# Routing wholly on VectorE in paced pieces, gate products over 48 instead of 64 tiles, and every fourth one-hot row made by ScalarE, in a two-layer float32 block

## The chip, the cores and the metric

The kernel runs on one core of a Trainium2 chip. The metric is the device time of one execution in microseconds. The kernel before was timed three times: 1633.87, 1632.1 and 1633.6 us, a median of 1633.6. A profiled execution took 1632.75 us, and its span from the first to the last instruction is 1631.0 us. All times of the trace below are counted from the start of that span.

## The reference, cut to what matters

Two layers over 256 frames of width 1024, all in float32. The change touches the PEER part of the first layer, in which each frame picks 16 of 16384 single-neuron experts for each of 8 heads:

```python
def peer(x, w_q, sub_k1, sub_k2, expert_u, expert_v):
    q = (xt @ w_q).reshape(T, 8, 2, 128)
    s1 = einsum('thd,kd->thk', q[:, :, 0], sub_k1)      # 128 scores per head and side
    s2 = einsum('thd,kd->thk', q[:, :, 1], sub_k2)
    v1, i1 = top_k(s1, 16); v2, i2 = top_k(s2, 16)
    cand = (v1[..., :, None] + v2[..., None, :])        # 16 x 16 sums
    vals, ci = top_k(cand, 16)
    idx = i1[ci // 16] * 128 + i2[ci % 16]              # the chosen experts
    gates = softmax(vals)
    h = einsum('tkd,td->tk', expert_u[idx], x)
    a = gelu(h) * gates
    return einsum('tk,tkd->td', a, expert_v[idx])
```

## The kernel before

**Dense experts.** No expert is gathered. The kernel computes the hidden value of all 16384 experts for all 256 frames, as 128 tiles of 128 experts, and multiplies it with a gate matrix that is zero wherever an expert was not chosen. The up pass (tile `ps_u`, lines 575 to 577) takes one weight tile of 128x1024 from memory for each expert tile; the down pass (`acc_v`, line 605) follows with another 128 weight tiles.

**Split weights.** Each float32 weight tile is split into a rounded high part `wh` (ScalarE, line 63) and the rest `wl` (VectorE, line 69), and three matmuls of 256 columns are made for each of 8 slices: 24 matmuls for an expert tile. `Stream.get` issues the split of the tile two places ahead at the start of a tile; the buffer for it comes free when TensorE has finished the tile before.

**Routing.** `route` (lines 1101 to 1161) is a generator. After each up tile `pump` runs it to its next `yield`, twice after every fourth tile. It makes the top 16 of each side (`top16`, lines 1083 to 1098, with VectorE's MAX8, FIND_INDEX8 and MATCH_REPLACE8), the top 16 of 50 candidate sums, and then, for each block of 128 frames, turns the candidate number into the two key numbers with one-hot arrays of 128x2048 elements: a comparison, a product and a sum for each. Three of these products are on GpSimd (lines 1135, 1141 and 1148), the rest is on VectorE. The first key number is a sum over slots of differences (`d1`); a separate sum (`base`, lines 1135 and 1144) gives the start of the slot. Two transposes (`jtp`, line 1158) and a copy (line 1159) give `jt`: first key number, second key number and gate of each choice, with a column for each frame. The scratch of the routing lies in `ha1` and `ha2`, the arrays that later hold the hidden values (rows 0 to 111 and 112 to 127).

**Gates.** A frame's gate matrix (128x128) is the product of two one-hot arrays, `o1` (scaled by the gate, VectorE, line 1179) and `o2` (GpSimd, line 1178). `g_step` handles four frames: `apply` multiplies the product of the step before into the hidden values that exist already (VectorE, line 1199) and copies the rest to where later hidden values will be (ScalarE, line 1201); `products` makes four float32 products (TensorE, line 1187) from the one-hot arrays of the step before; `build` makes the next four pairs of one-hot arrays. One `g_step` stands behind each up tile, so 256 frames take 64 tiles. `epilogue`, at the start of a tile, applies gelu to the tile before (ScalarE, lines 1209 and 1212) and multiplies the part whose gates are there (VectorE, line 1213).

**Order.** Nothing reorders these: each engine runs its instructions in the order in which the code above emits them, and semaphores alone hold it up. An up tile therefore emits, in this order, the split of the tile two ahead (lines 63, 69), the epilogue of the tile before, its 24 matmuls, a gate step, and a piece of the routing.

Of the kernel before, what the change touches and what calls it, by code (L numbers as in the profile page):

```python
# [15 lines left out]
ALU = mybir.AluOpType  # L16
# [147 lines left out]
class Kern:  # L164
# [404 lines left out]
    def mm_wstat(self, ps, w, xh, xl, nk=8, off=0):  # L569
# [375 lines left out]
    def experts(self, second):  # L945
# [11 lines left out]
        with tc.tile_pool(name="ha", bufs=1, side="right") as hp:  # L957
# [28 lines left out]
            self.bg.append(self.route(s, rb, self.slots, self.jt))  # L986
# [51 lines left out]
    def scores(self, xh, xl, kt, qt, s):  # L1038
# [16 lines left out]
        for side in range(2):  # L1055
            for h in range(4 - 4 * side, 8):
# [17 lines left out]
                self.pump()  # L1074
# [8 lines left out]
    def top16(self, jobs):  # L1083

        nc = self.nc
        for v, sc, ov, oi in jobs:
            nc.vector.max(ov[:, 0:8], v)
        for v, sc, ov, oi in jobs:
            nc.vector.max_index(oi[:, 0:8], ov[:, 0:8], v)
        for v, sc, ov, oi in jobs:  # L1090
            nc.vector.match_replace(sc, ov[:, 0:8], v, -3.0e38)
        yield
        for v, sc, ov, oi in jobs:
            nc.vector.max(ov[:, 8:16], sc)
        for v, sc, ov, oi in jobs:
            nc.vector.max_index(oi[:, 8:16], ov[:, 8:16], sc)
        yield

    def route(self, s, r, start, jt):
        nc = self.nc  # L1100
        for n in range(4):
            side, h0 = n // 2, 4 * (n % 2)
            while self.scored <= n:
                yield
            for b in range(NB):
                for h in range(h0, h0 + 4, 2):
                    yield from self.top16([(s[b][side][:, h + j], r["sc"][j], r["v"][b][:, side, h + j],
                                            r["iu"][b][:, side, h + j]) for j in range(2)])
        oh4 = r["oh"].rearrange("p (h k) e -> p h k e", k=16)
        oh24 = r["oh2"].rearrange("p (h k) e -> p h k e", k=16)  # L1110
        slots = lambda ap: ap[:, None, :].to_broadcast([P, P, 16])
        per = lambda ap: ap[:, :, None].to_broadcast([P, P, 16])
        for b in range(NB):
            v, fi, d1, cand = r["v"][b], r["fi"], r["d1"], r["cand"]
            for x in range(8):
                n, at = self.WIDTH[x], self.START[x]
                nc.vector.tensor_tensor(cand[:, :, at:at + n], v[:, 0, :, x:x + 1].to_broadcast([P, 8, n]),
                                        v[:, 1, :, 0:n], op=ALU.add)
            nc.vector.tensor_tensor(cand[:, :, 42:50], v[:, 0, :, 8:16], v[:, 1, :, 0:1].to_broadcast([P, 8, 8]),
                                    op=ALU.add)  # L1120
            yield
            nc.vector.tensor_copy(fi, r["iu"][b])
            nc.vector.tensor_copy(d1[:, :, 0:1], fi[:, 0, :, 0:1])
            nc.vector.tensor_tensor(d1[:, :, 1:16], fi[:, 0, :, 1:16], fi[:, 0, :, 0:15], op=ALU.subtract)
            yield
            for h in range(0, 8, 2):
                yield from self.top16([(cand[:, h + j], r["sc"][j][:, 0:50], r["cv"][:, h + j], r["ci"][:, h + j])
                                       for j in range(2)])
            g = r["out"][2].rearrange("p (h k) -> p h k", k=16)
            nc.vector.tensor_copy(r["cf"], r["ci"].rearrange("p h k -> p (h k)"))  # L1130
            nc.vector.tensor_tensor(g, r["cv"], r["cv"][:, :, 0:1].to_broadcast([P, 8, 16]), op=ALU.subtract)
            nc.scalar.activation(g, g, AF.Exp)
            yield
            nc.vector.tensor_tensor(r["oh"], per(r["cf"]), slots(start[:, 0]), op=ALU.is_ge)  # L1134
            nc.gpsimd.tensor_tensor(r["oh2"], r["oh"], slots(start[:, 1]), op=ALU.mult)  # L1135
            yield
            nc.vector.tensor_reduce(r["sm"], g, axis=AX.X, op=ALU.add)
# [11 lines left out]
            yield
            nc.vector.tensor_reduce(r["out"][0], r["oh"], axis=AX.X, op=ALU.add)  # L1150
            yield
            yield
            yield
            nc.vector.tensor_reduce(r["out"][1], r["oh2"], axis=AX.X, op=ALU.add)
            yield
            ps = self.psum("acc", f"jtp{b}", [P, 3, P])
            for j in range(3):
                nc.tensor.transpose(ps[:, j], r["out"][j], self.ident)
            nc.scalar.activation(jt[:, :, b * P:b * P + P], ps, AF.Copy)
            yield  # L1160
        self.route_done = True

    def experts_up(self, xh, xl, jt, pu):
# [61 lines left out]

        for i in range(P):
# [8 lines left out]
        self.drain()  # L1235
# [559 lines left out]
```

## Time and profile before

| what | value |
|---|---|
| median of three runs | 1633.6 us (1632.1 to 1633.87) |
| the profiled execution | 1632.75 us, span 1631.0 us |
| TensorE busy | 1583.3 us, 97% of the span |
| VectorE, ScalarE, GpSimd busy | 1121.7, 814.7 and 423.3 us |
| up tiles begin | at 254.0 us |
| gate steps, first and last product | at 437.9 and 675.2 us |
| down pass begins | at 697.7 us |

"Busy" of TensorE is a sum over pipelined matmuls and doesn't say that each of them ran at its best. What matters is where TensorE waits, for whom, and which engine's queue the work of that other engine stands behind. A profile's "idle before" in brackets is the time that an engine stood still ahead of an instruction, with the instruction whose end released it.

### The profile page before, as it was taken

The page shows a single profiled execution, that of the slowest core. Times are in us where ns is not written, and L with a number is a line of the kernel's source. Part 1 is how long each engine was busy: PE and PEld are TensorE (multiplying, and loading weights), DVE is VectorE, ACT ScalarE, POOL GpSimd, SP SyncE. Part 2 cuts the span into 40 slices and gives each one's busy share as a digit, 9 for nine tenths or more (in the row PEclk, how much of TensorE's full clock was granted, in tenths as well). Part 3 has the DMA queues.
Part 4 walks back from the last instruction along what each step waited for, and adds up shares of the span by engine and source line. Part 5 has one row for each costly group of instructions (what it writes and reads, how often), then busy time and mean ns, then how long its engine had stood idle before and what let it go on. Part 6 is the DMA issues. An engine that isn't in the chain of part 4 may idle for free.

```text
span 1631.0 us, 27358 instructions
## 1 busy us (share of the span) xinstructions
PE 1583.3 (97%) x10366; PEld 1439.3 (88%) x10366; DVE 1121.7 (69%) x2197; ACT 814.7 (50%) x1417; POOL 423.3 (26%) x462
## 2 busy tenths in 40 slices
PE   7999999989899999999999999999999989899998
PEld 6899899989899999988888888799997977689996
DVE  4477758898877788755555555755557879775555
ACT  5544545445344444455555555654446655564443
POOL 3121100041689999400000000021101574110000
PEclk9999999999999999999999999999999999999999
DMA  6555555546444444456666666566655532356563
GB/s 205 160 160 177 170 160 174 183 132 181 153 143 143 141 136 140 154 181 207 193 194 194 194 194 194 168 195 196 195 182 172 165 116 78 129 168 182 188 186 116
DMA packets 75667, 273.12 MB, mean 167 GB/s; under 512 B 8800, under 2 KB 8928, under 8 KB 75536
## 3 DMA queue, kind: packets, MB, share of 16 engines
q1 hardware_dynamic: 73728, 267.16, 52.9%
q0 software_dynamic: 1520, 3.93, 0.9%
q8 instruction: 82, 1.34, 0.3%
q14 instruction: 49, 0.40, 0.1%
q10 hardware_dynamic: 288, 0.29, 0.1%
HBM read 270.29 MB, written 1.05 MB: 166 GB/s over the span
## 4 chain that ended last, share of the span: by engine, by line
PE 87%; DVE 7%; ACT 2%; issue 2%; POOL 1%; DMA 0%; DVEq 0%; ACTq 0%
PE acc_v L605 21%; PE ps_u L577 7%; PE acc_ffn L605 7%; PE ps_u L576 7%; PE ps_u L575 7%; PE g L1187 3%; DVE wl L69 3%; PE acc_wo L605 2%; PE ffn2u L576 1%; PE ffn2u L575 1%; PE ffn2u L577 1%; PE ffn2g L576 1%; PE ffn2g L575 1%; PE ffn2g L577 1%; PE ffn1u L577 1%
## 5 line engine op out<-in xcount | busy, mean ns | idle before, releaser
L69 DVE TENSOR_TENSOR wl<-raw,wh 128x1024 fp32r<-128x1024 f32 x477 | 610.6, 1281 | 412.2 <-ACT wh L63 411.1
L63 ACT ACTIVATE wh<-raw 128x1024 fp32r<-128x1024 f32 x492 | 519.5, 1057 | 406.8 <-PE acc_v L605 166.7
L577 PE MATMUL ps_u<-xh_n,wl 128*128 128x256 f32 x1024 | 292.5, 286 | 9.6 <-DVE wl L69 9.6
L575 PE MATMUL ps_u<-xh_n,wh 128*128 128x256 f32 x1024 | 297.0, 290 | 0.0
L576 PE MATMUL ps_u<-xl_n,wh 128*128 128x256 f32 x1024 | 291.7, 285 | 0.0
L1178 POOL TENSOR_SCALAR o<-iota,jt 128x128 f32<-128x128 f32 x256 | 219.3, 872 | 29.4 <-PE g L1187 29.0
L577 PEld LDWEIGHTS ps_u<-xh_n,wl 128*128 128x128 f32 x1024 | 198.0, 193 | 10.6 <-DVE wl L69 10.6
L575 PEld LDWEIGHTS ps_u<-xh_n,wh 128*128 128x128 f32 x1024 | 198.7, 194 | 0.0
L576 PEld LDWEIGHTS ps_u<-xl_n,wh 128*128 128x128 f32 x1024 | 198.4, 194 | 0.0
L605 PE MATMUL acc_v<-wh,ah 128*128 128x512 f32 x508 | 157.6, 389 | 1.4 <-ACT ah L316 1.4
L605 PE MATMUL acc_v<-wl,ah 128*128 128x512 f32 x508 | 157.5, 389 | 0.0
L605 PE MATMUL acc_v<-wh,al 128*128 128x512 f32 x508 | 157.3, 389 | 0.0
L605 PEld LDWEIGHTS acc_v<-wh,ah 128*128 128x128 f32 x508 | 95.3, 188 | 21.3 <-ACT ah L316 1.6
L605 PEld LDWEIGHTS acc_v<-wl,ah 128*128 128x128 f32 x508 | 95.3, 188 | 19.9
L605 PEld LDWEIGHTS acc_v<-wh,al 128*128 128x128 f32 x508 | 95.3, 188 | 19.8
L362 POOL TENSOR_TENSOR ha<-res,final_g 128x512 f32<-128x512 f32 x3 | 3.9, 1293 | 311.4 <-DVE res L390 305.8
L1201 ACT ACTIVATE ha<-g 128x64 f32<-128x64 f32 (+53 forms) x118 | 22.4, 238 | 109.4 <-DVE ha L1199 109.4
L1179 DVE TENSOR_SCALAR o<-iota,jt 128x128 f32<-128x128 f32 x256 | 76.8, 363 | 0.0
L69 POOL TENSOR_TENSOR wl<-raw,wh 128x1024 fp32r<-128x1024 f32 x15 | 36.1, 2407 | 121.3 <-ACT wh L63 121.3
L1187 PE MATMUL g<-o,o 128*128 128x128 f32 x512 | 67.4, 274 | 0.0
L1187 PEld LDWEIGHTS g<-o,o 128*128 128x128 f32 x512 | 62.6, 192 | 0.0
L1135 POOL TENSOR_TENSOR ha<-ha,slots 128x2048 f32<-128x2048 f32 x2 | 10.9, 5457 | 177.1 <-DVE ha L1134 177.1
(615 smaller groups left out, 3488.2 us busy)
## 6 DMA issues: line engine op xcount, KB each, us to landing
raw<-in_u_dram SPq DMA_DIRECT2D x128, 512.0 KB, 3.5
raw<-in_v_dram SPq DMA_DIRECT2D x128, 512.0 KB, 3.5
raw<-in_ffn_gu_dram SPq DMA_DIRECT2D x88, 512.0 KB, 3.9
raw<-in_w_in_dram SPq DMA_DIRECT2D x74, 512.0 KB, 3.6
raw<-in_ffn_d_dram SPq DMA_DIRECT2D x44, 512.0 KB, 3.5
raw<-in_w_out_dram SPq DMA_DIRECT2D x20, 512.0 KB, 3.5
raw<-in_wq_dram SPq DMA_DIRECT2D x16, 512.0 KB, 3.6
raw<-in_w_ab_dram SPq DMA_DIRECT2D x8, 512.0 KB, 3.4
```

Source lines behind the costliest of these rows:

```text
L63: self.k.nc.scalar.activation(h, self.raw[i], AF.Copy)
L69: (eng or self.k.nc.vector).tensor_sub(lo, self.raw.pop(i), h.bitcast(F32))
L362: ("Pool", 1.3, lambda: nc.gpsimd.tensor_tensor(o, x, y, op=ALU.mult))], deps)
L575: nc.tensor.matmul(ps, h[:, c], xh[:, k], start=(k == 0), stop=False)
L576: nc.tensor.matmul(ps, h[:, c], xl[:, k], start=False, stop=False)
L577: nc.tensor.matmul(ps, lo[:, c], xh[:, k], start=False, stop=(k == nk - 1))
L605: nc.tensor.matmul(acc[b][hf], (ah, ah, al)[p][:, s], (h, lo, h)[p][:, c], start=first and p == 0, stop=last and p == 2)
L1135: nc.gpsimd.tensor_tensor(r["oh2"], r["oh"], slots(start[:, 1]), op=ALU.mult)
L1178: nc.gpsimd.tensor_scalar(o2[:, j], self.iota, jt[:, 1, t:t + 1], None, op0=ALU.is_equal)
L1179: nc.vector.tensor_scalar(o1[:, j], self.iota, jt[:, 0, t:t + 1], jt[:, 2, t:t + 1], op0=ALU.is_equal, op1=ALU.mult)
L1187: nc.tensor.matmul(ps[:, j], o2[:, j], o1[:, j], start=True, stop=True)
L1201: nc.scalar.activation(ha[:, m - a:e - a, t0:t0 + GB], pv[:, m:e], AF.Copy)
```

## The change

1. The routing generator is no longer in the list that `pump` runs. It yields an estimate of its VectorE time, and `pace(1.5)` after each score tile and each up tile runs it until 1.5 us of work are used up (`None` ends a turn at once).
2. The three GpSimd products are gone. Every one-hot step is on VectorE, in halves of 128x1024 elements. The extra sum for `base` is gone: the differences carry 256 times the slot's start, so that one sum holds the key number and the start, and four small instructions take them apart. Two small conversions move to ScalarE.
3. `g_step` is called after every third quarter of a tile (through a hook in `mm_wstat`), four times in three tiles: 256 frames in 48 tiles.
4. Of each four frames the fourth pair of one-hot arrays is made by ScalarE, with two Abs and two Relu; VectorE and GpSimd make three each.

```diff
+    def pace(self, us):
+        self.credit = min(self.credit, us) + us
+        while self.slow and self.credit > 0:
+            c = next(self.slow, "end")
+            if c == "end":
+                self.slow = None
+            elif c is None:
+                break
+            else:
+                self.credit -= c
...
             if k == nk // 2 - 1:
                 self.half()
+            if hook and k % 2 and k < nk - 1:
+                hook()
...
-            nc.vector.tensor_tensor(r["oh"], per(r["cf"]), slots(start[:, 0]), op=ALU.is_ge)
-            nc.gpsimd.tensor_tensor(r["oh2"], r["oh"], slots(start[:, 1]), op=ALU.mult)
...
-            nc.gpsimd.tensor_tensor(oh4, oh4, d1[:, :, None, :].to_broadcast([P, 8, 16, 16]), op=ALU.mult)
...
-            nc.vector.tensor_reduce(r["base"], r["oh2"], axis=AX.X, op=ALU.add)
...
+            for c in HALF:
+                oh = r["oh"][:, c]
+                vec.tensor_tensor(oh, per(cf, c), slots(start[:, 0]), op=ALU.is_ge)
+                yield 1.2
+                vec.tensor_tensor(heads(oh), heads(oh), by_head(d1, c), op=ALU.mult)
+                yield 1.2
+                vec.tensor_reduce(pack[:, c], oh, axis=AX.X, op=ALU.add)
+                yield 1.2
...
+            vec.tensor_scalar(base, pack, 1.0 / 256, 12582912.0, op0=ALU.mult, op1=ALU.add)
...
+                if j == 3:
+                    nc.scalar.activation(o2[:, j], self.iota, AF.Abs, scale=-1.0, bias=jt[:, 1, t:t + 1])
+                    nc.scalar.activation(o1[:, j], self.iota, AF.Abs, scale=-1.0, bias=jt[:, 0, t:t + 1])
+                    nc.scalar.activation(o2[:, j], o2[:, j], AF.Relu, scale=-1.0, bias=1.0)
+                    nc.scalar.activation(o1[:, j], o1[:, j], AF.Relu, scale=self.ng[:, t // 4:t // 4 + 1],
+                                         bias=jt[:, 2, t:t + 1])
+                    continue
...
-            self.mm_wstat(pss[i], w, xh, xl)
-            g_step()
-            self.pump(1 + (i % 4 == 3))
+            self.mm_wstat(pss[i], w, xh, xl, hook=quarter)
+            quarter()
+            self.pace(1.5)
```

In the changed program the routing of the first and second block ends (`jtp`) in the 49th and 71st up tile, where it ended in the 37th and 55th. The 64 products stand in the tiles 75 to 122, where they stood in 58 to 121. No load of an activation table is added.

What VectorE has in a row in the one-hot part of the routing, before (lines 1134 to 1154 are the routing, line 69 the split of a weight tile; a wait on `Pool` is one on GpSimd):

```order
L69 TENSOR_TENSOR wl104_3709<-raw104_3565,wh104_3708 128x1024 [waits DMAHW4_49,PE_49,Activation_49]
L1137 TENSOR_REDUCE ha1_2116<-ha2_2117 128x8
L1138 RECIPROCAL ha1_2116<-ha1_2116 128x8 [waits DVE_49]
L1139 TENSOR_TENSOR ha2_2117<-ha2_2117,ha1_2116 128x128 [waits DVE_49]
L69 TENSOR_TENSOR wl105_3744<-raw105_3601,wh105_3743 128x1024 [waits DMAHW5_49,PE_49,Activation_49]
L69 TENSOR_TENSOR wl106_3777<-raw106_3639,wh106_3776 128x1024 [waits DMAHW6_49,PE_49,Activation_49]
L1144 TENSOR_REDUCE ha2_2117<-ha2_2117 128x128 [waits Pool_49]
```

And now, at the same place:

```order
L69 TENSOR_TENSOR wl112_3965<-raw112_3821,wh112_3964 128x1024 [waits DMAHW4_49,PE_49,Activation_49]
L1162 TENSOR_TENSOR ha1_2117<-ha2_2118,slots_87 128x1024
L1164 TENSOR_TENSOR ha1_2117<-ha1_2117,ha2_2118 128x1024 [waits DVE_49]
L1166 TENSOR_REDUCE ha2_2118<-ha1_2117 128x64 [waits DVE_49]
L69 TENSOR_TENSOR wl113_4000<-raw113_3859,wh113_3999 128x1024 [waits DMAHW5_49,PE_49,Activation_49]
L1162 TENSOR_TENSOR ha1_2117<-ha2_2118,slots_87 128x1024
```

The sums waited for GpSimd with splits queued around them; now the product stands on VectorE itself and the only waits are on VectorE's own results.

ScalarE in the middle of the gate steps, before, one tile and the start of the next (line 63 is the split, 1209 and 1212 the gelu, 1201 the copies of `apply`):

```order
L63 ACTIVATE wh172_6812<-raw172_6604 128x1024 [waits DMAHW0_49,PE_49]
L1209 ACTIVATE ha1_2116<-ps_u96_6769 128x100 [waits PE_49]
L1212 ACTIVATE gt96_6819<-ps_u96_6769 128x156 [waits Activation_49]
L1201 ACTIVATE ha1_2116<-g156_6797 128x15x4 [waits DVE_49]
L1201 ACTIVATE ha2_2117<-g156_6797 128x16x4
L63 ACTIVATE wh173_6865<-raw173_6657 128x1024 [waits DMAHW1_49,PE_49]
```

And now, from the copies of one tile with two gate steps to the next split (lines 1212 to 1215 are the Abs and Relu, 1241 the copies):

```order
L1241 ACTIVATE ha1_2117<-g124_6711 128x14x4 [waits DVE_49]
L1241 ACTIVATE ha2_2118<-g124_6711 128x16x4
L1212 ACTIVATE o2_132_6765<-iota_81,jt_86 128x128 [waits Pool_49]
L1213 ACTIVATE o1_132_6766<-iota_81,jt_86 128x128
L1214 ACTIVATE o2_132_6765<-o2_132_6765 128x128 [waits Activation_49]
L1215 ACTIVATE o1_132_6766<-o1_132_6766,jt_86,ng_120 128x128 [waits Activation_49]
L1241 ACTIVATE ha1_2117<-g128_6760 128x14x4 [waits DVE_49]
L1241 ACTIVATE ha2_2118<-g128_6760 128x16x4
L1212 ACTIVATE o2_136_6803<-iota_81,jt_86 128x128 [waits Pool_49]
L1213 ACTIVATE o1_136_6804<-iota_81,jt_86 128x128
L1214 ACTIVATE o2_136_6803<-o2_136_6803 128x128 [waits Activation_49]
L1215 ACTIVATE o1_136_6804<-o1_136_6804,jt_86,ng_120 128x128 [waits Activation_49]
```

Four instructions stand between the copies of a gate step and the next split on ScalarE.

VectorE at the same place now (line 1253 is the epilogue's product, 1239 the product of `apply`, 1219 the one-hot arrays):

```order
L69 TENSOR_TENSOR wl173_6741<-raw173_6504,wh173_6740 128x1024 [waits DMAHW1_49,PE_49,Activation_49]
L1253 TENSOR_TENSOR ha1_2117<-ha1_2117,gt97_6747 128x124 [waits Activation_49]
L1239 TENSOR_TENSOR ha1_2117<-ha1_2117,g124_6711 128x98x4
L1219 TENSOR_SCALAR o1_132_6766<-iota_81,jt_86 128x128 [waits DVE_49]
L1219 TENSOR_SCALAR o1_132_6766<-iota_81,jt_86 128x128 x2
L1239 TENSOR_TENSOR ha1_2117<-ha1_2117,g128_6760 128x98x4 [waits PE_49]
L1219 TENSOR_SCALAR o1_136_6804<-iota_81,jt_86 128x128 [waits DVE_49]
L1219 TENSOR_SCALAR o1_136_6804<-iota_81,jt_86 128x128 x2
L69 TENSOR_TENSOR wl174_6816<-raw174_6559,wh174_6815 128x1024 [waits DMAHW2_49,PE_49,Activation_49]
```

In a tile with one gate step there is one line 1239 and three of line 1219; the order is otherwise that of before, with three one-hot arrays for four.

## Rows read from the trace of the kernel before

**Rows 1.** Busy time of TensorE, and the chain of work that ended last by engine, from the page.

```profile
PE 1583.3 (97%) x10366; PEld 1439.3 (88%) x10366; DVE 1121.7 (69%) x2197; ACT 814.7 (50%) x1417; POOL 423.3 (26%) x462
...
PE 87%; DVE 7%; ACT 2%; issue 2%; POOL 1%; DMA 0%; DVEq 0%; ACTq 0%
```

**Rows 2.** Busy time by stretch of the up tiles: stretch, its length, busy us and (instructions) of TensorE, of its weight loads, of VectorE, ScalarE and GpSimd, granted TensorE clock, DMA share, GB/s.

```profile
345.00:435.00 90.00, 80.06 (x620) 78.82 (x620) 79.87 (x123) 37.00 (x56) 36.46 (x14) 0.94 0.51 153
437.00:673.00 236.00, 236.00 (x2008) 236.00 (x2007) 193.10 (x446) 109.57 (x304) 211.54 (x248) 1.00 0.46 142
254.00:335.00 81.00, 81.00 (x678) 81.00 (x677) 69.79 (x297) 40.65 (x59) 0.00 (x0) 1.00 0.58 182
```

**Rows 3.** VectorE in order of time in the one-hot part of the routing: start, us, line, operation.

```profile
340.01 1.22 DVE L69 TENSOR_TENSOR wl<-raw,wh 128x1024 fp32r<-128x1024 f32 x1
...
341.70 4.23 DVE L1139 TENSOR_TENSOR ha<-ha,ha 128x128 f32<-128x128 f32 x1
345.85 6.75 DVE L69 TENSOR_TENSOR wl<-raw,wh 128x1024 fp32r<-128x1024 f32 x2
```

**Rows 4.** GpSimd in the same stretch.

```profile
340.40 5.38 POOL L1135 TENSOR_TENSOR ha<-ha,slots 128x2048 f32<-128x2048 f32 x1 [141.65 <-DVE ha L1134]
345.86 5.66 POOL L1141 TENSOR_TENSOR ha<-ha,ha 128x2048 f32<-128x2048 f32 x1
```

**Rows 5.** TensorE's waits in the up tiles (engine, line, for whom: us in total, times, longest).

```profile
PE ps_u L577 <- DVE wl L69: 9.6, 5, 2.4
```

**Rows 6.** From the chain of work in order of time, 340 to 375 us: one matmul before the first stall and one behind it.

```profile
343.06 0.12 PE ps_u L577
...
355.52 0.21 PE ps_u L576
```

**Rows 7.** VectorE's routing instructions by line and shape, 300 to 1000 us: busy us, mean ns of one.

```profile
L1134 DVE TENSOR_TENSOR ha<-ha,slots 128x2048 f32<-128x2048 f32 x2 | 4.6, 2286 | 0.0
...
L1144 DVE TENSOR_REDUCE ha<-ha 128x128 f32<-128x2048 f32 x2 | 4.5, 2273 | 0.0
...
L1089 DVE FIND_INDEX8 ha<-ha 128x8 uint32<-128x128 f32 x6 | 1.6, 285 | 0.0
...
L1091 DVE MATCH_REPLACE8 ha<-ha 128x128 f32<-128x128 f32 x6 | 1.6, 274 | 0.0
...
L1094 DVE MAX8 ha<-ha 128x8 f32<-128x128 f32 x6 | 1.4, 279 | 0.0
...
L1091 DVE MATCH_VALUE_LOAD ha<-ha 128x8 f32 x6 | 0.4, 74 | 0.0
```

**Rows 8.** ScalarE in order of time in the middle of the gate steps: start, us, line, operation, and in brackets the idle time before it and who ended it.

```profile
588.47 1.06 ACT L63 ACTIVATE wh<-raw 128x1024 fp32r<-128x1024 f32 x1 [0.28 <-PE ps_u L576]
589.43 0.23 ACT L1209 ACTIVATE ha<-ps_u 128x96 f32<-128x96 f32 x1
589.56 0.30 ACT L1212 ACTIVATE gt<-ps_u 128x160 f32<-128x160 f32 x1
591.63 0.33 ACT L1201 ACTIVATE ha<-g 128x56 f32<-128x56 f32 x2 [1.77 <-DVE ha L1199]
592.24 1.06 ACT L63 ACTIVATE wh<-raw 128x1024 fp32r<-128x1024 f32 x1 [0.27 <-PE ps_u L576]
```

**Rows 9.** VectorE in the same stretch.

```profile
587.74 1.25 DVE L1179 TENSOR_SCALAR o<-iota,jt 128x128 f32<-128x128 f32 x4
589.56 1.23 DVE L69 TENSOR_TENSOR wl<-raw,wh 128x1024 fp32r<-128x1024 f32 x1 [0.57 <-ACT wh L63]
590.72 0.41 DVE L1213 TENSOR_TENSOR ha<-ha,gt 128x160 f32<-128x160 f32 x1
591.04 0.55 DVE L1199 TENSOR_TENSOR ha<-ha,g 128x392 f32<-128x392 f32 x1
```

**Rows 10.** ScalarE's splits in an early and a late gate step.

```profile
505.60 1.06 ACT L63 ACTIVATE wh<-raw 128x1024 fp32r<-128x1024 f32 x1 [0.39 <-PE ps_u L576]
...
660.04 1.06 ACT L63 ACTIVATE wh<-raw 128x1024 fp32r<-128x1024 f32 x1
...
663.48 0.21 ACT L1201 ACTIVATE ha<-g 128x44 f32<-128x44 f32 x1 [2.05 <-DVE ha L1199]
663.80 1.06 ACT L63 ACTIVATE wh<-raw 128x1024 fp32r<-128x1024 f32 x1
```

**Rows 11.** The gate products in the chain of work of the whole span, the first, one in the middle and the last of 64: start, us.

```profile
437.89 0.89 PE g L1187 x8
...
592.32 0.89 PE g L1187 x8
...
675.18 0.89 PE g L1187 x8
```

**Rows 12.** ScalarE's splits in two up tiles that follow each other without a gate step, each held up by TensorE alone.

```profile
343.46 1.06 ACT L63 ACTIVATE wh<-raw 128x1024 fp32r<-128x1024 f32 x1 [1.50 <-PE ps_u L576]
...
346.34 1.06 ACT L63 ACTIVATE wh<-raw 128x1024 fp32r<-128x1024 f32 x1 [1.55 <-PE ps_u L576]
```

**Rows 13.** ScalarE instructions of 128x128 elements: an exponential with a bias column (line 1512, in order of time, with the instruction behind it), the same without a column (1132) and a copy (1537), by line and shape: busy us, mean ns.

```profile
1355.47 0.39 ACT L1512 ACTIVATE at_p<-at_p,at_st 128x128 f32<-128x128 f32 x1
1355.77 0.19 ACT L1512 ACTIVATION_READ_ACCUMULATOR at_p<-at_p,at_st 128x1 f32 x1
...
L1132 ACT ACTIVATE ha<-ha 128x128 f32<-128x128 f32 x2 | 0.6, 311 | 0.9 <-DVE ha L1131 0.8
...
L1537 ACT ACTIVATE at<-at_v 128x128 f32<-128x128 f32 x8 | 2.1, 264 | 2.3 <-PE at_v L1535 2.2
```

**Rows 14.** VectorE's weight split with GpSimd idle (260 to 340 us) and beside GpSimd's one-hot arrays (440 to 480 us), by line, and GpSimd's arrays themselves, from the page: busy us, mean ns.

```profile
L69 DVE TENSOR_TENSOR wl<-raw,wh 128x1024 fp32r<-128x1024 f32 x27 | 33.0, 1222 | 10.3 <-ACT wh L63 10.0
...
L69 DVE TENSOR_TENSOR wl<-raw,wh 128x1024 fp32r<-128x1024 f32 x11 | 13.6, 1233 | 9.7 <-ACT wh L63 9.7
...
L1178 POOL TENSOR_SCALAR o<-iota,jt 128x128 f32<-128x128 f32 x256 | 219.3, 872 | 29.4 <-PE g L1187 29.0
```

**Rows 15.** Busy time by stretch in the second layer's mixer, columns as in rows 2.

```profile
1310.00:1320.00 10.00, 8.58 (x73) 8.38 (x72) 9.27 (x11) 4.54 (x5) 10.00 (x8) 1.00 0.36 108
...
1330.00:1340.00 10.00, 6.93 (x45) 5.97 (x44) 6.85 (x20) 2.52 (x8) 9.29 (x6) 0.86 0.39 115
```

More of the change, by code (lines that the diff above doesn't have):

```diff
@@ L1107, in route @@
                     yield from self.top16([(s[b][side][:, h + j], r["sc"][j], r["v"][b][:, side, h + j],
[L1108 to L1112, printed above, removed]
+                                            r["iu"][b][:, side, h + j]) for j in range(2)], 1.0)
@@ L1113, in route @@
+        HALF = [slice(0, 64), slice(64, P)]
+        slots = lambda ap: ap[:, None, :].to_broadcast([P, 64, 16])
+        per = lambda ap, c: ap[:, c, None].to_broadcast([P, 64, 16])
+        by_head = lambda ap, c: ap[:, c.start // 16:c.stop // 16, None, :].to_broadcast([P, 4, 16, 16])
+        heads = lambda ap: ap.rearrange("p (h k) e -> p h k e", k=16)
         for b in range(NB):
             v, fi, d1, cand = r["v"][b], r["fi"], r["d1"], r["cand"]
+            nc.scalar.activation(fi, r["iu"][b], AF.Copy)
@@ L1124, in route @@
[L1124 to L1125 removed]
+                vec.tensor_tensor(cand[:, :, at:at + n], v[:, 0, :, x:x + 1].to_broadcast([P, 8, n]),
+                                  v[:, 1, :, 0:n], op=ALU.add)
+                if x % 4 == 3:
+                    yield 0.9
+            vec.tensor_tensor(cand[:, :, 42:50], v[:, 0, :, 8:16], v[:, 1, :, 0:1].to_broadcast([P, 8, 8]), op=ALU.add)
+            yield 0.3
@@ L1126, in route @@
+            vec.tensor_copy(d1[:, :, 0:1], fi[:, 0, :, 0:1])
+            vec.tensor_tensor(d1[:, :, 1:16], fi[:, 0, :, 1:16], fi[:, 0, :, 0:15], op=ALU.subtract)
+            vec.tensor_tensor(d1, d1, start[:, None, 1].to_broadcast([P, 8, 16]), op=ALU.add)
+            yield 0.8
             for h in range(0, 8, 2):
                 yield from self.top16([(cand[:, h + j], r["sc"][j][:, 0:50], r["cv"][:, h + j], r["ci"][:, h + j])
-                                       for j in range(2)])
+                                       for j in range(2)], 0.75)
@@ L1149, in route @@
[L1149 to L1155, printed above, removed]
+            yield None
+            for c in HALF:
[6 more added lines that the diff above has]
+                yield 1.2
@@ new lines, in route @@
+            vec.tensor_reduce(r["sm"], g, axis=AX.X, op=ALU.add)
+            vec.reciprocal(r["sm"], r["sm"])
+            vec.tensor_tensor(g, g, r["sm"][:, :, None].to_broadcast([P, 8, 16]), op=ALU.mult)
+            yield 0.8
+            vec.tensor_scalar(base, pack, 1.0 / 256, 12582912.0, op0=ALU.mult, op1=ALU.add)
+            vec.tensor_scalar(base, base, 12582912.0, None, op0=ALU.subtract)
+            vec.scalar_tensor_tensor(pack, base, -256.0, pack, op0=ALU.mult, op1=ALU.add)
+            vec.tensor_sub(base, cf, base)
@@ L1156, in route @@
+            yield 1.0
+            for c in HALF:
+                oh = r["oh2"][:, c]
+                vec.tensor_tensor(oh, per(base, c), slots(self.iota[:, 0:16]), op=ALU.is_equal)
+                yield 1.2
+                vec.tensor_tensor(heads(oh), heads(oh), by_head(fi[:, 1], c), op=ALU.mult)
+                yield 1.2
+                vec.tensor_reduce(r["out"][1][:, c], oh, axis=AX.X, op=ALU.add)
+                yield 1.2
+            yield None
+            yield None
             ps = self.psum("acc", f"jtp{b}", [P, 3, P])
@@ L1224, in g_step, with quarter @@
                 nxt += GB
+        n = 0
+        def quarter():
+            nonlocal n
+            n += 1
+            if n % 3 == 0:
+                g_step()
         for i in range(P):
```

55 lines of the change are left out of this document (23 added, 32 removed).

## The prediction

> **What bounds the kernel now.** The busy times and the chain come first [rows 1]: TensorE is busy in 97% of the span, and the chain that ends last is 87% TensorE. So a change elsewhere pays only where TensorE waits, and costs only where it makes TensorE wait. The next view is the up pass by stretches [rows 2]. With neither gate steps nor one-hot sums (254 to 335 us) TensorE runs 678 instructions in 81.0 us, 8.37 per us; that is a tile of 24 in 2.88 us, which is also the distance of two splits that wait for TensorE alone [rows 12]. In the gate steps (437 to 673 us) there is no wait either: the first and the last of 64 products lie 237.29 us apart, 3.767 us for a tile [rows 11], so the four products cost 3.767 - 2.88 = 0.89 us. Only the stretch from 345 to 435 us falls short: at 8.37 per us its 90 us hold 753 instructions, and 620 are there. The missing 133 are 15.9 us.
>
> Where they went: TensorE's waits in the up tiles are 9.6 us, for the low part of a weight tile [rows 5]. VectorE takes 6.75 us for two splits that begin at 345.85, and 4.23 us for a small product at 341.70 [rows 3], just while GpSimd runs its two large products [rows 4]; a split takes 1.22 us otherwise. The remaining 6 us follow the waits: a matmul takes 0.12 us before the stall and 0.21 us behind it [rows 6], with a mean granted clock of 0.94 over the stretch [rows 2], a mixture of the levels 2.4 and 1.2 GHz.
>
> **The change part by part.** *Routing without GpSimd.* The three GpSimd products for each block go, and with them what held VectorE up: **-15.9 us**, if VectorE's new share fits. It is declared as 1.5 us a tile. The rows give for a top-16 of two heads 2 x (2 x 0.279 + 2 x 0.285 + 0.274 + 3 x 0.074) = 3.25 us where 3.3 are declared, and 2.286 / 2 = 1.14 us for a half of a one-hot step where 1.2 are [rows 7]. With the split of 1.22 us that is at most 2.7 us in a tile of 2.88. It fits, narrowly; 0.18 us x some 65 tiles leave 12 us of room. The product with a broadcast row on VectorE is not in the trace: between 1.14 (the comparison of the same size) and twice that, 8 of them cost up to 9 us more, which the room hides. I take no cost. The small ScalarE conversions stand a turn ahead of their readers, and ScalarE is half idle there [rows 2].
>
> *The later end of the routing* (second block in tile 71 instead of 55) moves the gate steps to the tiles 75 to 122. They still end ahead of the down pass, so this costs nothing. TensorE's own work is unchanged: 64 products at 0.89 us, wherever they stand.
>
> *Gate steps, four in three tiles.* TensorE needs 3 x 2.88 + 4 x 0.89 = 12.2 us for three tiles. The question is whether ScalarE and VectorE deliver in that time, and here their order counts, not their busy shares. Look at one tile of before, from split to split on ScalarE [rows 8, 9]: the high split begins at 588.47; the low split waits for it until 589.56; VectorE then does the epilogue's product (590.72) and that of the gate step (591.04); ScalarE's copies wait 1.77 us for that one and begin at 591.63; behind them stands the next high split. This is a closed loop: each step waits for the one before, through two engines' queues, and no prefetch loosens it. It took 3.77 us only because the last step waited 0.27 us for TensorE. By itself it takes 3.50 us, in an early step 3.77 - 0.39 = 3.38 us, and in a late one 3.65 us (663.48 + 0.21 - 660.04) [rows 8, 10]. TensorE was the bound by some 0.1 to 0.4 us a tile.
>
> The change puts Abs, Abs, Relu, Relu between the copies and the next high split, inside this loop. An instruction of 128x128 with one column operand takes 0.39 us, and the one behind it begins after 0.30; without a column 0.31 [rows 13]. Two columns (the last Relu) are not in the trace: 0.31 + 2 x 0.08 = 0.47 us by the difference. So the Abs begin at 0 and 0.30, the first Relu at 0.60, the second, which needs the second Abs (ends at 0.69), at 0.81 behind the first, and the next split at 0.81 + 0.37 = **1.18 us**. The Abs can begin 0.10 us before the copies end, as neighbours on ScalarE overlap (589.43 + 0.23 against 589.56) [rows 8]. A tile with one gate step becomes 3.50 + 1.18 - 0.10 = 4.58 us. The second step of a double tile adds copies and four instructions once more, 0.33 - 0.10 + 1.18 = 1.41 us; VectorE's three one-hot arrays and second product run beside that. Three tiles take 3 x 4.58 + 1.41 = 15.15 us in the middle, 14.8 early and 15.5 late. As fewer gates are done when an expert tile has the same number, the epilogue's products are shorter than in these rows, by up to 0.07 us; I take 15.05. Against 12.2 that is **+2.85 us for three tiles**. 64 steps, of which the first applies nothing, make some 15.5 such groups: 44.2 us. One part is free: the one-hot arrays were ready at 588.99 (587.74 + 1.25) and used at 592.32 [rows 9, 11], so the lag costs nothing until 3.3 us are used up. That leaves **+40.9 us**.
>
> Bounds of the added chain: if all four were as short as the cheapest instruction of this size (0.264 us [rows 13]) and began 0.15 us apart where they may, it would be 0.6 us, and the whole part 15.5 x (2.85 - 4 x 0.58) - 3.3 = +4.9 us. Without any overlap it is 0.39 + 0.39 + 0.31 + 0.47 = 1.56 us, and the part +64 us. The instruction with a column is the nearest row, so 1.18 stands.
>
> The Trainium skill, "ScalarE: Activation LUTs", section "What ACT_TABLE_LOAD costs", has a price for what no row shows: 186 ns plus 0.833 ns per element plus about 93 ns for each column operand, 0.48 us for the last Relu; the sum by it would be the same within 1 us.
>
> *GpSimd beside VectorE in the gate steps* stays: three arrays four times in three tiles, as four arrays once a tile. The low split takes 1.233 us beside it and 1.222 without [rows 14], so nothing is added. The Trainium skill, "SBUF — State Buffer", section "SBUF: two separate sides", has a rule that speaks against it: a VectorE instruction with two SBUF inputs and a GpSimd one that reads SBUF exclude each other for a whole instruction. By that rule the time would be that of the last rival below. The large products of rows 4 behave so; the one-hot arrays of rows 14 do not.
>
> **The sum.** 1632.75 us (span 1631.0) - 15.9 + 40.9 = **1657.7 us** against the profiled execution, which lies 0.85 us under the median of the three runs. I say 1657.
>
> **The rivals.** *TensorE stays the bound.* ScalarE's four instructions are so short, or so much of the loop overlaps, that the stall of the routing is all that changes. Place: the loop of rows 8 and 9. It ends not slower if the added chain is under 0.78 us (there 15.5 x 1.25 - 3.3 = 16 us are lost and 16 won), and at 0.47 us or less the loop fits in 12.2 us: 1616.8 us; at the lower bound above 1621.7. For it: by busy time alone neither engine is full (82% and 46% of the gate steps [rows 2]). Against it: the waits in rows 8 to 10 show the loop with 0.1 to 0.4 us to spare, and two column instructions alone take 0.6 us. Chance 0.13, and 0.05 for a tie between.
>
> *The clock falls in the gate steps.* With waits of 0.7 us in each step TensorE is busy some 82%. A stretch busy 69% had a granted clock of 0.86, one at 86% had 1.00 [rows 15], and a matmul at the lower level takes 0.21 us, a tile 5.1 us, more than the loop. Ten of the 48 tiles at that level would add about 10 us: 1668 us. Chance 0.1.
>
> *VectorE is overfull in the routing.* If its pieces cost more than declared by over 0.18 us a tile, TensorE waits for the splits there; 0.1 us more in 65 tiles gives +6.5 us, 1664 us. Chance 0.05.
>
> *GpSimd's one-hot arrays hold the splits up.* One takes 0.87 us; if a split in the loop lost half of one, 48 tiles would lose 21 us more: 1678 us. Rows 14 show 0.01 us and not 0.44. Chance 0.02.
>
> That the products don't come in 48 tiles is excluded by the program's order.
>
> **How the numbers follow.** Forecast 0.65, clock 0.1, overfull VectorE 0.05, GpSimd 0.02, together slower 0.82; tie 0.05; faster 0.13 (0.2%, or 3.3 us, is about what a measurement of this kernel can tell from no change). The range leaves out the faster cases and the upper bound's far end: a chain between 0.85 and 1.4 us gives 1637 to 1671, and the clock reaches to the same end. So 1637 to 1672.
>
> **What would show it.** Right: no wait for line 69's result between 254 and 465 us and a clock of 1.00; from the 75th tile TensorE's waits are on the one-hot arrays (VectorE's or ScalarE's), about 41 us in all; three tiles take 15 us; the Abs take 0.39 us; ScalarE never waits for TensorE before a split there. The up pass then takes 469 us instead of 443.7. Wrong: 12.2 us for three tiles, splits that still wait for TensorE, or TensorE waiting ahead of tile 75.

## The result and the profile after

The changed kernel takes 1652.53 us (median of 4, 1652.02 to 1654.26) where the kernel before takes 1632.85 (1631.69 to 1633.87): a ratio of 1.0123, 95% interval 1.0105 to 1.014, slower by 19.7 us. The profiled execution took 1652.02 us (span 1650.3); the forecast was 1657.

The busy shares hardly tell anything: TensorE has 97% as before [rows 1]. From the page, busy time and chain by engine:

```profile
PE 1594.9 (97%) x10366; PEld 1441.6 (87%) x10366; DVE 1080.7 (65%) x2139; ACT 881.0 (53%) x1660; POOL 315.8 (19%) x392
...
PE 85%; DVE 6%; ACT 5%; POOL 2%; issue 2%; DMA 0%; DVEq 0%; ACTq 0%; POOLq 0%
```

In the chain of work that ended last, ScalarE's share rose from 2% to 5%. The stretches say where; columns as in [rows 2]:

```profile
345.00:435.00 90.00, 90.00 (x753) 90.00 (x752) 70.67 (x175) 48.36 (x73) 4.92 (x6) 1.00 0.58 180
468.00:695.00 227.00, 208.19 (x1633) 197.22 (x1632) 146.71 (x353) 150.46 (x499) 140.82 (x186) 1.00 0.35 110
```

In the routing's stretch TensorE now runs 753 instructions in 90 us at a clock of 1.00, just the number worked out for a stretch without a stall. The down pass begins at 717.9 us, 463.7 us behind the first up tile (443.7 before). In the gate steps it runs 1633 in 227 us (7.19 per us), where it ran 2008 in 236 (8.51) [rows 2]; the clock is 1.00 there too. TensorE's waits from 195 to 730 us, at matmuls and at weight loads:

```profile
PE g L1227 <- DVE o L1219: 9.4, 18, 0.7
...
PE g L1227 <- POOL o L1218: 5.4, 8, 0.9
...
PE g L1227 <- ACT o L1215: 2.0, 8, 0.3
...
PEld g L1227 <- POOL o L1218: 18.8, 25, 1.0
PEld g L1227 <- ACT o L1215: 9.6, 30, 0.5
```

No wait for line 69 is left [rows 5]. All that is new stands at the gate products. The arrays of all three makers are named, GpSimd's for the most time (24.2 us of 45.2); that GpSimd is not the cause is shown below by the run that keeps its arrays and moves ScalarE's, in which no gate product waits. ScalarE in order of time shows why the step as a whole is late, from the split of a tile with two gate steps to that of the next (line 63 the split, 1249 and 1252 the gelu, 1241 the copies of `apply`, 1212 to 1215 Abs, Abs, Relu, Relu):

```profile
582.66 1.05 ACT L63 ACTIVATE wh<-raw 128x1024 fp32r<-128x1024 f32 x1
583.61 0.27 ACT L1249 ACTIVATE ha<-ps_u 128x132 f32<-128x132 f32 x1
583.77 0.27 ACT L1252 ACTIVATE gt<-ps_u 128x124 f32<-128x124 f32 x1
585.67 0.33 ACT L1241 ACTIVATE ha<-g 128x56 f32<-128x56 f32 x2 [1.63 <-DVE ha L1239]
585.89 0.40 ACT L1212 ACTIVATE o<-iota,jt 128x128 f32<-128x128 f32 x1
586.18 0.40 ACT L1213 ACTIVATE o<-iota,jt 128x128 f32<-128x128 f32 x1
586.48 0.30 ACT L1214 ACTIVATE o<-o 128x128 f32<-128x128 f32 x1
586.68 0.49 ACT L1215 ACTIVATE o<-o,jt,ng 128x128 f32<-128x128 f32 x1
587.06 0.32 ACT L1241 ACTIVATE ha<-g 128x56 f32<-128x56 f32 x2
...
588.43 1.06 ACT L63 ACTIVATE wh<-raw 128x1024 fp32r<-128x1024 f32 x1
...
591.47 0.33 ACT L1241 ACTIVATE ha<-g 128x52 f32<-128x52 f32 x2 [1.65 <-DVE ha L1239]
...
592.85 1.05 ACT L63 ACTIVATE wh<-raw 128x1024 fp32r<-128x1024 f32 x1
...
597.26 1.05 ACT L63 ACTIVATE wh<-raw 128x1024 fp32r<-128x1024 f32 x1
```

The splits lie 5.77, 4.42 and 4.41 us apart, 14.60 us for three tiles, and none of them has a wait for TensorE in brackets, as they had before [rows 8]. ScalarE still stands idle 1.63 us in each tile, waiting for VectorE's product. VectorE between the same two splits waits for ScalarE in turn:

```profile
583.75 1.23 DVE L69 TENSOR_TENSOR wl<-raw,wh 128x1024 fp32r<-128x1024 f32 x1 [1.59 <-ACT wh L63]
584.89 0.28 DVE L1253 TENSOR_TENSOR ha<-ha,gt 128x124 f32<-128x124 f32 x1
585.09 0.56 DVE L1239 TENSOR_TENSOR ha<-ha,g 128x392 f32<-128x392 f32 x1
```

The high split starts the low split; VectorE's two products follow it; these start ScalarE's copies; and behind the copies and the four instructions stands the next high split. Two engines that each wait 1.6 us for the other, with no other engine named in their brackets: that is what a closed loop looks like in this trace.

### The profile page after: what moved, and what is told of

Read it like the earlier page. It is cut to its first block, busy times and chain, and to the rows that moved or that the text cites. A ratio compares the mean times of both kernels' runs of the same rounds, so it can differ in the third digit from the quotient of the medians.

```text
span 1650.3 us, 27460 instructions
## 1 busy us (share of the span) xinstructions
PE 1594.9 (97%) x10366; PEld 1441.6 (87%) x10366; DVE 1080.7 (65%) x2139; ACT 881.0 (53%) x1660; POOL 315.8 (19%) x392
## 4 chain that ended last, share of the span: by engine, by line
PE 85%; DVE 6%; ACT 5%; POOL 2%; issue 2%; DMA 0%; DVEq 0%; ACTq 0%; POOLq 0%
PE acc_v L621 21%; PE acc_ffn L621 7%; PE ps_u L589 7%; PE ps_u L590 7%; PE ps_u L591 7%; PE g L1227 3%; PE acc_wo L621 2%; DVE wl L69 1%; PE ffn2u L590 1%; PE ffn2u L589 1%; PE ffn2u L591 1%; PE ffn2g L590 1%; PE ffn2g L589 1%; PE ffn2g L591 1%; PE ffn1u L591 1%
## 5 line engine op out<-in xcount | busy, mean ns | idle before, releaser
L69 DVE TENSOR_TENSOR wl<-raw,wh 128x1024 fp32r<-128x1024 f32 x477 | 596.2, 1250 | 473.8 <-ACT wh L63 472.9
L1218 POOL TENSOR_SCALAR o<-iota,jt 128x128 f32<-128x128 f32 x192 | 145.7, 774 | 348.9 <-ACT jt L1191 198.4
L621 PEld LDWEIGHTS acc_v<-wl,ah 128*128 128x128 f32 x508 | 95.4, 188 | 19.7
L1227 PE MATMUL g<-o,o 128*128 128x128 f32 x512 | 80.1, 289 | 18.8 <-DVE o L1219 9.4
L1227 PEld LDWEIGHTS g<-o,o 128*128 128x128 f32 x512 | 66.9, 190 | 29.8 <-POOL o L1218 18.8
L1241 ACT ACTIVATE ha<-g 128x140 f32<-128x140 f32 (+37 forms) x114 | 20.3, 224 | 81.1 <-DVE ha L1239 80.9
L1219 DVE TENSOR_SCALAR o<-iota,jt 128x128 f32<-128x128 f32 x192 | 57.1, 351 | 0.0
L331 DVE TENSOR_TENSOR al<-ha,ah 128x256 fp32r<-128x256 f32 x128 | 53.1, 417 | 0.5 <-ACT ah L330 0.5
```

What stands on the lines that cost most here:

```text
L69: (eng or self.k.nc.vector).tensor_sub(lo, self.raw.pop(i), h.bitcast(F32))
L331: self.nc.vector.tensor_sub(dl, src, dh.bitcast(F32))
L621: nc.tensor.matmul(acc[b][hf], (ah, ah, al)[p][:, s], (h, lo, h)[p][:, c], start=first and p == 0, stop=last and p == 2)
L1219: nc.vector.tensor_scalar(o1[:, j], self.iota, jt[:, 0, t:t + 1], jt[:, 2, t:t + 1], op0=ALU.is_equal, op1=ALU.mult)
L1227: nc.tensor.matmul(ps[:, j], o2[:, j], o1[:, j], start=True, stop=True)
L1241: nc.scalar.activation(ha[:, m - a:e - a, t0:t0 + GB], pv[:, m:e], AF.Copy)
```

## The experiments

The theory is the prediction's: the stall of the routing goes (-16 us), and the four ScalarE instructions lengthen a loop through two queues, which takes the bound from TensorE. The rivals: ScalarE's added work is harmless and the density of the steps costs; ScalarE's total work costs, wherever it stands; the terms don't add. The kernel before, timed again beside the runs, had medians of 1633.35 us (the first four runs) and 1632.42 us (the last three).

**ScalarE's arrays alone** on the kernel before:

```diff
+                if j == 3:
+                    (Abs, Abs, Relu, Relu as in the change)
+                    continue
...
```

Not shown are the negated gates that the last Relu reads; ScalarE makes them with one copy for each block of frames.

> The kernel before (its routing, one gate step per up tile, 64 tiles), and ScalarE makes every fourth pair of one-hot arrays with Abs, Abs, Relu, Relu; nothing else is changed. Theory of the loop (the four instructions stand between the copies of a gate step and the next high split, in a loop that runs through ScalarE's and VectorE's queues): a gate-step tile takes 3.4 + 1.1 = 4.4 to 4.5 us where TensorE needs 3.77; 64 tiles lose 40 to 46 us, of which about 3 are hidden: 1670 to 1680 us, and a high split no longer waits for TensorE. Rival (the four instructions fill ScalarE's idle half, and what costs is that the steps stand closer together): the time stays within 5 us of the kernel before, 1633 us.

Measured: 1666.85 us, ratio 1.0208 (1.0191 to 1.0225). ScalarE's splits of the middle, every line 63 in the order of time:

```profile
585.81 1.05 ACT L63 ACTIVATE wh<-raw 128x1024 fp32r<-128x1024 f32 x1
...
590.23 1.05 ACT L63 ACTIVATE wh<-raw 128x1024 fp32r<-128x1024 f32 x1
...
594.64 1.05 ACT L63 ACTIVATE wh<-raw 128x1024 fp32r<-128x1024 f32 x1
```

A tile takes 4.41 to 4.42 us and no split waits for TensorE. The arrays cost 33.5 us with the steps at their old density: the mechanism is the theory's, the time 3 us below its range (the profiled execution, with 1670.04 us, is inside it; the other three took 1666.7 to 1667.01).

**No array on ScalarE**, the change else whole:

```diff
-                if j == 3:
-                    (Abs, Abs, Relu, Relu)
-                    continue
```

> The changed kernel without ScalarE's one-hot arrays: VectorE and GpSimd make all four pairs of a gate step, which still stand four in three tiles, with the new routing. Theory of the loop: with the four instructions gone the loop of a tile takes 3.3 to 3.4 us again, three tiles with a double step some 11.5; TensorE needs 12.2, and GpSimd's 16 arrays for three tiles need 12.4 (0.77 us each) to 14.0 (0.87), so GpSimd becomes the bound: 1617 to 1645 us, most likely 1630. Rival (the density of the steps is what costs): it stays at the changed kernel's 1652 us within 5 us.

Measured: 1619.32 us, 0.9918 (0.9901 to 0.9934). The density costs, at most, the 2.5 us by which this run lies above the next one; that rival, which had 1652 us, is out. GpSimd came close to being the bound without becoming it: its row from 468 to 660 us shows 188.6 of the 192 us busy, with 0.78 us for an array where 0.77 to 0.87 were taken, 12.5 us for 16. Over 15.5 groups of three tiles that is 4.7 us more than TensorE needs, of which the head start of 3.3 covers most. No gate product waits in this trace.

```profile
L1211 POOL TENSOR_SCALAR o<-iota,jt 128x128 f32<-128x128 f32 x248 | 188.6, 779 | 68.7 <-PE g L1220 68.4
```

**The same four instructions, ahead of the copies** instead of behind them:

```diff
+        def begin(t0):
+            (o2, o1; Abs, Abs, Relu, Relu)
...
+            new = begin(nxt) if self.route_done and nxt < T else None
             if prod:
                 apply()
             if built:
                 products()
-            if self.route_done and nxt < T:
-                build(nxt)
+            if new:
+                build(nxt, *new)
...
```

> The changed kernel with the same work, but in each gate step ScalarE's Abs, Abs, Relu, Relu are issued ahead of the copies of apply instead of behind them, so that they stand where ScalarE waits for VectorE's product, and the copies are followed at once by the next high split. Theory of the loop: it is the place of the four instructions that costs, not their work; a single-step tile takes 3.3 to 3.5 us, a double tile some 1.4 more, three tiles 11.5, less than TensorE's 12.2; TensorE is the bound again and the time falls to 1617 to 1622 us, below both kernels, with high splits that wait for TensorE. Rival (ScalarE's total of work, or its contention with VectorE, is what costs): three tiles still take 14.6 us and the time stays at 1652 us within 5 us.

Measured: 1616.83 us, 0.9901 (0.9885 to 0.9918), faster than both kernels. ScalarE in one tile (1251 and 1254 gelu, 1210 to 1213 the four, 1243 the copies):

```profile
585.88 1.06 ACT L63 ACTIVATE wh<-raw 128x1024 fp32r<-128x1024 f32 x1 [0.30 <-PE ps_u L590]
586.85 0.24 ACT L1251 ACTIVATE ha<-ps_u 128x104 f32<-128x104 f32 x1
586.98 0.29 ACT L1254 ACTIVATE gt<-ps_u 128x152 f32<-128x152 f32 x1
587.16 0.40 ACT L1210 ACTIVATE o<-iota,jt 128x128 f32<-128x128 f32 x1
587.45 0.40 ACT L1211 ACTIVATE o<-iota,jt 128x128 f32<-128x128 f32 x1
587.75 0.30 ACT L1212 ACTIVATE o<-o 128x128 f32<-128x128 f32 x1
587.95 0.49 ACT L1213 ACTIVATE o<-o,jt,ng 128x128 f32<-128x128 f32 x1
588.95 0.32 ACT L1243 ACTIVATE ha<-g 128x36 f32<-128x36 f32 x2 [0.52 <-DVE ha L1241]
589.65 1.06 ACT L63 ACTIVATE wh<-raw 128x1024 fp32r<-128x1024 f32 x1 [0.38 <-PE ps_u L590]
```

The work is the same to the instruction, and each takes as long as before. They now lie in the stretch in which ScalarE waited for VectorE, whose rest is 0.52 us, and the splits wait for TensorE again (two of three; the one behind a double step doesn't). 35.7 us hung on the place of four instructions in a queue; ScalarE's total work, as a rival, falls, and so does GpSimd, whose arrays are the same. This is the fastest of the kernels; its trace names no wait of TensorE at the up tiles or the gate products.

**The old routing under the new gate steps** (the routing's part of the diff taken back):

```diff
-            self.slow = self.route(s, rb, self.slots, self.jt)
+            self.bg.append(self.route(s, rb, self.slots, self.jt))
...
-                self.pace(1.5)
+                self.pump()
...
-            self.pace(1.5)
+            self.pump(1 + (i % 4 == 3))
...
```

> The changed kernel's gate steps (four in three tiles, every fourth pair on ScalarE) on the routing of the kernel before, with its large products on GpSimd. If the two terms are independent, as the sum has them: the stall of some 16 us at 345 to 435 us returns and the 14.6 us for three gate-step tiles stay, 1652.5 + 16 = 1668 us (1665 to 1671). Rival (the routing's change has another effect, for example through the later place of the gate steps, so that the terms don't add): outside of 1662 to 1674 us.

Measured: 1668.76 us, 1.0219 (1.0202 to 1.0236): 16.2 us above the changed kernel. The terms add. In the stretch of the stall 613 instructions run, about as few as before [rows 2]:

```profile
345.00:435.00 90.00, 79.44 (x613) 78.02 (x612) 78.84 (x120) 38.28 (x61) 35.19 (x12) 0.94 0.49 148
```

**Half of ScalarE's part in the loop** (Abs and Relu of the second key; VectorE makes the other array):

```diff
                 if j == 3:
                     nc.scalar.activation(o2[:, j], self.iota, AF.Abs, scale=-1.0, bias=jt[:, 1, t:t + 1])
-                    nc.scalar.activation(o1[:, j], self.iota, AF.Abs, ...)
                     nc.scalar.activation(o2[:, j], o2[:, j], AF.Relu, scale=-1.0, bias=1.0)
-                    nc.scalar.activation(o1[:, j], o1[:, j], AF.Relu, ...)
-                    continue
-                nc.gpsimd.tensor_scalar(o2[:, j], ...)
+                else:
+                    nc.gpsimd.tensor_scalar(o2[:, j], ...)
```

> The changed kernel, but of each fourth pair ScalarE makes only the second-key array (Abs, Relu), at the same place, and VectorE makes the other: half of ScalarE's added instructions in the loop. Theory of the loop, from the rows of the runs so far: the copies take the queue 0.24 us, the Abs must end (0.40) before the Relu, and the split starts 0.2 behind the Relu's start, so 0.61 us are added where the four instructions add 1.15; a single-step tile takes 3.26 + 0.61 = 3.87 us, the second step of a double tile 1.67 (VectorE's four arrays 1.17 and the product 0.5), three tiles 13.28 against TensorE's 12.2: 15.5 x 1.08 - 3.3 = +13 on 1617: 1630 us (1625 to 1637), and three tiles measure 13.0 to 13.6. Rival (what costs is that ScalarE takes part in the pairs at all, through the semaphores between the engines, and not the length of what it does in the loop): 1645 us or more.

Measured: 1632.95 us, 1.0004 against the kernel before (0.9994 to 1.0014). Splits:

```profile
580.55 1.04 ACT L63 ACTIVATE wh<-raw 128x1024 fp32r<-128x1024 f32 x1
...
584.44 1.04 ACT L63 ACTIVATE wh<-raw 128x1024 fp32r<-128x1024 f32 x1
...
589.15 0.32 ACT L1238 ACTIVATE ha<-g 128x44 f32<-128x44 f32 x2 [0.64 <-DVE ha L1236]
...
590.01 1.04 ACT L63 ACTIVATE wh<-raw 128x1024 fp32r<-128x1024 f32 x1
...
593.91 1.04 ACT L63 ACTIVATE wh<-raw 128x1024 fp32r<-128x1024 f32 x1
```

13.36 us for three tiles, and 15.5 x 1.16 - 3.3 = 14.7 us above 1616.8 is 1631.5. A tile with one step takes 3.89 us (forecast 3.87), against 4.41 with all four instructions. The second step of the double tile adds 1.68 us (5.57 - 3.89), and there ScalarE waits 0.64 us for VectorE, which now makes four arrays: that part is VectorE's length, not ScalarE's. So the cost follows the length of what stands in the loop, on either engine: nothing of the four in it, half and all of them give 1619, 1633 and 1652 us. The rival, 1645 us or more, is out. The prediction's tie stood at 1.25 us lost for three tiles; here 1.16 are lost, and the time is that of the kernel before.

**The routing alone**: one step for each tile, no array on ScalarE.

```diff
-                if j == 3:
-                    (Abs, Abs, Relu, Relu)
-                    continue
...
-            self.mm_wstat(pss[i], w, xh, xl, hook=quarter)
-            quarter()
+            self.mm_wstat(pss[i], w, xh, xl)
+            g_step()
```

> The new routing alone: one gate step behind each up tile as before, and no one-hot array on ScalarE. Theory: the stall at 345 to 435 us is gone (no waits there, clock 1.00), but the steps begin in tile 75 and one for each tile does not fit into the 53 that are left: some 11 steps stand exposed behind the last up tile, each as long as GpSimd's four arrays (3.1 to 3.5 us), of which TensorE's 0.89 us had to be done anyway: 1617 + 11 x 2.4 = 1643 us, up to 1655 with a lower clock behind the wait. So the later end of the routing is free only with denser gate steps. Rival (the late end costs nothing by itself, the steps overlap with the start of the down pass): 1617 to 1622 us.

Measured: 1631.47 us, 0.999 (0.998 to 0.9999), 12 us below the forecast. The mechanism is there: from 671.5 us on TensorE has gate products alone, and the down pass begins at 695.06. Busy time of that stretch (columns as in [rows 2]) and GpSimd in it:

```profile
671.50:695.00 23.50, 21.19 (x81) 16.97 (x80) 18.28 (x59) 0.41 (x2) 21.14 (x36) 0.62 0.02 10
...
671.69 21.14 POOL L1211 TENSOR_SCALAR o<-iota,jt 128x128 f32<-128x128 f32 x36 [0.39 <-PE g L1220]
```

The exposed steps take 4 x 0.587 = 2.35 us each, where 3.1 to 3.5 were taken from arrays beside a split. GpSimd sets their time (21.14 of 23.50 us busy), while TensorE's granted clock, with waits between its products, is 0.62. So the later end of the routing is free only because the gate steps stand closer; alone it costs 14.6 us (against 1616.83) and eats nearly all of the 16 that the new routing wins.

**The large products on VectorE, whole**, in the kernel before:

```diff
-            nc.gpsimd.tensor_tensor(r["oh2"], r["oh"], slots(start[:, 1]), op=ALU.mult)
+            nc.vector.tensor_tensor(r["oh2"], r["oh"], slots(start[:, 1]), op=ALU.mult)
```

and the same for the two others.

> The kernel before with one edit: the three large one-hot products of the routing, on GpSimd before, stand on VectorE, whole (128x2048), in the same turns. Gates as before. Theory (the stall came from GpSimd's products holding VectorE's splits up): most of the 15.9 us is won; the turns in which VectorE now has a comparison and a product of 2.3 us each and the split of 1.22 need 5.8 us in a tile of 2.88 and cost 1 to 2 us, four times: 1620 to 1626 us, with no instruction of VectorE over 2.4 us. Rival (the stall came from the size of the pieces and their order, which stay): 1630 to 1636 us.

Measured: 1625.22 us, 0.9957 (0.994 to 0.9973). The products take 2.29 us on VectorE (5.4 to 5.7 on GpSimd [rows 4]), a split takes 1.22 us again, and the clock stays at 1.00; but 61 of 753 instructions are still missing in the stretch, and from 336 to 440 us TensorE still waits 4.8 us for the low part of a weight tile:

```profile
345.00:435.00 90.00, 84.52 (x692) 82.84 (x691) 78.44 (x140) 41.53 (x65) 11.79 (x13) 1.00 0.57 175
...
338.07 2.28 DVE L1134 TENSOR_TENSOR ha<-ha,slots 128x2048 f32<-128x2048 f32 x1
340.39 2.29 DVE L1135 TENSOR_TENSOR ha<-ha,slots 128x2048 f32<-128x2048 f32 x1
342.60 1.22 DVE L69 TENSOR_TENSOR wl<-raw,wh 128x1024 fp32r<-128x1024 f32 x1
...
PE ps_u L577 <- DVE wl L69: 4.8, 5, 2.5
```

Two large instructions in one turn hold VectorE for 4.5 us (338.07 to 342.60), more than a tile of 2.88, before the next split. Taking the products from GpSimd alone is worth 7.2 us (1632.42 - 1625.22; 4.4 to 9.8 by the interval). The rest of the 16 comes with the halves, the pacing and the merged sum together; which of them brings how much was not tried.

## Why the prediction was right

**The stall: right, to the instruction.** 753 were worked out, 753 ran. With the stall gone and the loop harmless the prediction gave 1616.8 us; the run with ScalarE's work ahead of the copies took 1616.83 (an agreement closer than its own runs, 1616.52 to 1618.4, so partly luck), and the old routing under the new gates is 16.2 us above the changed kernel where 15.9 were taken. What the prediction left out is that leaving GpSimd does only half of this: with whole products on VectorE about half of the stall stays, and the halves and the pacing are needed for the rest.

**VectorE's share of the routing: right.** No wait for a split is left. The product with a broadcast row (line 1164), for which up to 2.28 us were allowed, takes 1.22 us.

**The later end of the routing: right in this kernel,** and 15 us of cost without the denser steps.

**The loop: right mechanism, 5 us too long.** The means of the four instructions, 460 to 700 us:

```profile
L1215 ACT ACTIVATE o<-o,jt,ng 128x128 f32<-128x128 f32 x64 | 31.1, 487 | 0.0
L1212 ACT ACTIVATE o<-iota,jt 128x128 f32<-128x128 f32 x64 | 25.7, 402 | 0.0
L1213 ACT ACTIVATE o<-iota,jt 128x128 f32<-128x128 f32 x64 | 25.5, 399 | 0.0
L1214 ACT ACTIVATE o<-o 128x128 f32<-128x128 f32 x64 | 19.5, 305 | 0.0
```

Forecast were 0.39, 0.39, 0.31 and 0.47. The Trainium skill, "ScalarE: Activation LUTs", section "What ACT_TABLE_LOAD costs", has a formula by which the last one was estimated at 0.48 us; the trace agrees, with 487 ns. In a single-step tile the split follows the copies by 1.38 us (591.47 to 592.85), against 0.32 before [rows 10]: 1.06 us added, forecast 1.08. The second step of a double tile adds 1.39 (copies at 585.67 and 587.06), forecast 1.41. The term that was mis-sized is the loop without them: a single-step tile takes 4.41 us where 4.55 were taken. Most of that is the epilogue's product, 0.28 us for 124 columns; before, it took 0.37 at this width:

```profile
556.82 0.37 DVE L1213 TENSOR_TENSOR ha<-ha,gt 128x124 f32<-128x124 f32 x1
```

What makes it shorter now was not tried. Three tiles are therefore 14.60 us in the middle and not 15.05 (14.26 early, from 481.81 us, and 15.10 late, from 671.34 us, where the prediction had 14.8 and 15.5), and 15.5 x 2.4 - 3.3 = 33.9 us follow instead of 40.9; measured are 35.7 above 1616.8. This term takes off 7.0 us, more than the 4.5 us by which the forecast was too long; the 1.8 us between 33.9 and 35.7 are not located and happened to bring the forecast nearer.

**The waits: place right, makers in part.** They stand at the gate products alone, 16.8 us at matmuls and 28.4 at weight loads (the second-key array is the loaded operand; weight loads overlap matmuls, so the sum of the two is not the loss). The prediction had named VectorE's and ScalarE's arrays; GpSimd's is named 33 times, ScalarE's 38 and VectorE's 18.

**The rivals.** The clock stayed at 1.00 in the gate steps, VectorE was not overfull, and no split was held up by GpSimd. That TensorE would stay the bound failed on the length that the prediction gave as its condition: 1.06 us are added to a tile with one step (1.16 in the prediction's count, which has the overlap of 0.10 still in it), where 0.47 would fit and 0.78 break even. Those two figures let the second step of a double tile shrink with ScalarE's work alone. The run with half of that work shows the limit: there the second step is VectorE's, 1.68 us with four arrays, and the time is already that of the kernel before.

## What to carry to other kernels

An engine's idle time lies at certain places in its queue; work put elsewhere in the queue can't use it. Before giving work to a half-idle engine, follow its queue for one period: if it waits for an engine that in turn waits for it, all that stands behind its wait and ahead of what the other engine waits for adds to the period, and the same work ahead of the waiting instruction is free as far as it fits into the wait (here 1.63 us). A piece of background work on the engine that feeds TensorE should be no longer than the slack of one tile, and when background work ends later, count the steps that follow it against the tiles that are left.

## What the hardware showed unexpectedly

GpSimd's one-hot arrays lose time beside VectorE's split, while the split loses hardly any. Rows of GpSimd in the changed kernel, three arrays each:

```profile
583.47 2.66 POOL L1218 TENSOR_SCALAR o<-iota,jt 128x128 f32<-128x128 f32 x3 [1.16 <-PE g L1227]
587.87 1.76 POOL L1218 TENSOR_SCALAR o<-iota,jt 128x128 f32<-128x128 f32 x3 [1.74 <-PE g L1227]
```

The first three meet the split of 583.75, the second three none until their end (the next one waits for ScalarE's high part, from 588.43 to 589.49): 0.90 us more. One by one, the second of the first three begins under the split, at 584.05 us, and takes 1.50 us; it ends 0.57 us behind the split (584.98), while its neighbours take 0.60 us each. Without a split beside it an array takes 0.587 us here and in the run of the routing alone (1.76 / 3 and 21.14 / 36), while the split takes 1.23 us beside arrays and 1.22 without [rows 14]. The Trainium skill, "SBUF — State Buffer", section "SBUF: two separate sides", says that a VectorE instruction with two SBUF inputs and a GpSimd one that reads SBUF exclude each other for a whole instruction, and that the one that starts first has its way. The trace agrees for the array that begins under the split: it waits the split out. It doesn't agree for the split: that of 583.75 begins while the first array (583.47 to 584.07) runs, and takes 1.23 us all the same. The large GpSimd products of [rows 4] did hold the splits: with them on VectorE a split takes 1.22 us. What decides who waits was not tried.
